# Moving a convolution block ahead of the last pair of heads, and conv work beside the second triangular solve

## The chip, the core and the metric

The kernel runs on one NeuronCore of a Trainium2 chip, in one launch and in float32. Its engines are TensorE (PE, matmuls and transposes), VectorE (DVE), ScalarE (ACT), GpSimd (POOL) and SyncE (SP, which issues most transfers; ACT issues some). Each engine works through its own instructions in a fixed order and waits on semaphores for the others. The metric is the device time of one execution in microseconds (us); a profile of one execution shows the span from its first to its last instruction, in the same unit.

## What is computed

One decoder layer for a sequence of 1024 tokens and a width of 1024. Its inputs meet in one projection, whose columns feed two groups side by side: an RWKV-7 group of 8 heads of 64, and a convolution group of 512 channels.

```
h = rmsnorm(x);  p = h @ w_in
y_rwkv: token shift, decays, then per head
    S_t = S_{t-1} (diag(decay_t) + a_t b_t^T) + v_t k_t^T ;  y_t = S_t r_t
    group norm, bonus, gate
y_conv: u * sigmoid(g), causal convolution with 31 taps, layer norm, silu
x = x + concat(y_rwkv, y_conv) @ w_out
x = x + relu(rmsnorm(x) @ w_ff1)^2 @ w_ff2
y = rmsnorm(x)
```

## The kernel before

Tokens lie in 16 chunks of 64. The recurrence is turned into small matrix products per chunk, for which a triangular system must be solved. The work comes in these parts; the names are those of the functions in the code.

- `mix_block` and `in_proj`: a block of 128 columns of the input projection, in two halves of 512 tokens. Each half takes 48 matmuls of 128x256 (three products of rounded halves of float32, eight slices of the width, two pieces). Eight heads make four pairs; each pair needs three such blocks (k, r and v). While the recurrence runs, their accumulators are the PSUM banks `cb` and `yb`, in turn.
- `conv_block`: two such blocks (value and gate) for 128 channels, so four halves. The product with the gate goes to the tile `h2`, of which there is one (`H2B = 1`); its first instruction is a memset of a border (`h` in the profile, L309). The convolution is 47 multiply-adds on DVE (`taps`, L328 to L331) and a join, which `do_taps(n)` issues in portions of n/31 of them. The weights of a block are loaded to one raw buffer and split by ACT and DVE (`load_w`, L219, L220).
- `decays` and `stage1`: for one pair and one half of the sequence, the decays, scaled keys (`AR`, `KB`), their products with a mask (`AM`, L471), and transposed copies, which are stored to DRAM for the recurrence (`lk_d`, `am_d`, `v_d`, `n2_d`).
- `solve`: for a group g of two pairs, DVE loads `Q` from `am_d`, inverts 128 small triangles of 32 in 60 steps (L528, L530) and stores them to `qd_d`. `merge` joins the triangles by two rounds of small products on PE (`QT,MX` and `QS,PT`) and stores the result to `th_d`.
- `step(g)`: one chunk of the recurrence of group g. `fetch` loads `LK`, `rhs` and `TA`; `chain` then runs hops of four matmuls of 64x64 on PE (eight in the trace): `rhs,LK`, a copy `SR` on ACT, `SR,TA` (the product with Th), a copy `rhs` on ACT, `rhs,LK` again and a sum on DVE (L624). Two more hops write the output. Group 0 uses the banks `ca` and `ya`, group 1 `cb` and `yb`. Each group has 16 chunks.
- `conv_norm(h)`: the layer norm and silu of the convolution for one half of the tokens; transposes on PE, the rest on ACT and DVE. It needs all taps of all four blocks. Its pool `sc` is opened and closed around it.
- `load_wout`: output weights, through two raw buffers (`woraw`, `RB = 2`), rounded by ACT (`woh`, L716) and completed by DVE (`wol`, L717). `out_first(t, n)`: 24 matmuls of 128x256 for the conv half of the output projection of 128 tokens and 512 columns; DVE adds the input (L724). `out_second(t)` adds the head half, after `post(d)` has normed and gated the recurrence's output.
- Then come the MLP (`early`, `Pair`) and its second product; they are not touched.

The order of the instructions on each engine is found when the kernel is built: a scheduler takes the operations in the order of the code as their priority and places each where its operands are expected to be there. `solve` and `merge` of both groups and `step(0)` stand one level (`HP = 4000`) ahead of their place, `step(1)` two levels. So the code's order of calls decides what is at hand when an engine would wait. Taps that are issued after a `solve` in the code are placed behind its last step (`gate`).

Of the kernel before, what the change touches and what calls it, by code (L numbers as in the profile page):

```python
# [52 lines left out]
def hymba_layer(ctx: ExitStack, tc: tile.TileContext, a: dict, out: bass.AP):  # L53
# [85 lines left out]
    cv_ctx = tc.tile_pool(name="cv", bufs=1)  # L139
# [41 lines left out]
    def prm(name, i=0, n=1):  # L181
        j, o = off[name]
        return pars[j][:, o + i:o + i + n]
# [30 lines left out]
    def load_w(c0):  # L214
        raw = wp.tile([P, 8, P], F32, name="wraw", bufs=1)
        nc.sync.dma_start(out=raw, in_=w_in_d[:, :, c0:c0 + P])
        wh = wp.tile([P, 8, P], F32R, name="wh")
        wl = wp.tile([P, 8, P], F32R, name="wl")
        S.activation(wh, raw, AF.Copy)  # L219
        V.tensor_tensor(wl, raw, wh.bitcast(F32), op=ALU.subtract)  # L220
        return wh, wl
# [80 lines left out]
    taps = []  # L302
    gate = {"solve": None}

    def conv_block(cb):
        tag = in_banks[-1]
        wg, wu = load_w(CG + cb * P), load_w(CU + cb * P)
        h2 = hc.tile([P, 3, 16 + 512], F32, name="h2", bufs=H2B)
        V.memset(h2[:, :, 0:16], 0.0)  # L309
        for h in range(2):  # L310
            bg = in_proj(wg, h * 512, 512, tag)
            th = hc.tile([P, 512], F32, name="th", bufs=1)
            S.activation(th, bg, AF.Tanh, scale=0.5)
            bu = in_proj(wu, h * 512, 512, tag)
            o = slice(16 + h * 256, 16 + h * 256 + 256)
            V.scalar_tensor_tensor(h2[:, 0:2, o].rearrange("p e n -> p n e"), th.rearrange("p (n e) -> p n e", e=2), 1.0,
                                   bu.rearrange("p (n e) -> p n e", e=2), op0=ALU.add, op1=ALU.mult)
            V.tensor_tensor(h2[:, 2, o], h2[:, 0, o], h2[:, 1, o], op=ALU.add)
        acc = accs[cb] = cv.tile([P, 2, 512], F32, name="acc", bufs=4)
        odd = mp.tile([P, 513], F32, name="odd", bufs=1)  # L320

        def tap(ph, i):

            o, c = ((acc[:, 0], cw[:, 2 * i, cb:cb + 1]), (odd[:, 1:513], cw[:, max(2 * i - 1, 0), cb:cb + 1]), (acc[:, 1], cws[:, i, cb:cb + 1]))[ph]
            x = h2[:, ph, i + 1:i + 1 + 512]
            if ph == 1 and i == 1:
                V.memset(odd[:, 0:1], 0.0)
                return V.tensor_scalar(o, x, c, None, op0=ALU.mult)  # L328
            if i == 0:
                return V.tensor_scalar(o, x, c, prm("conv_b", cb) if ph == 0 else cb2[:, cb:cb + 1], op0=ALU.mult, op1=ALU.add)  # L330
            return V.scalar_tensor_tensor(o, x, c, o, op0=ALU.mult, op1=ALU.add)  # L331

        def join(*_):
            V.tensor_tensor(acc[:, 1], acc[:, 1], acc[:, 0], op=ALU.subtract)
            V.tensor_tensor(acc[:, 1], acc[:, 1], odd[:, 1:513], op=ALU.subtract)
            return V.tensor_tensor(acc[:, 0], acc[:, 0], odd[:, 0:512], op=ALU.add)

        taps.extend((tap, (ph, i)) for ph in (0, 2, 1) for i in range(ph == 1, 16))
        taps.append((join, ()))
# [3 lines left out]
    def do_taps(n):  # L343
        tapped[0] += n
        for f, j in taps[:tapped[0] * 48 // TAPS - tapped[1]]:
            i = f(*j)
            if gate["solve"] is not None:
                tc.add_manual_dep(i.ins, gate["solve"].ins.name, NOSYNC, reason="solve first")
        n = tapped[0] * 48 // TAPS - tapped[1]
        tapped[1] += n  # L350
        del taps[:n]
# [3 lines left out]
    def mix_block(blk, hs):  # L355
        w = load_w(blk * P)
        for h in hs:
            pm = m0.tile([P, 513], F32, name="pm")
            if h == 0:
                V.memset(pm[:, 0:1], 0.0)  # L360
            else:
                S.copy(pm[:, 0:1], carry[:, blk:blk + 1])
            mx = mp.tile([P, 512], F32, name="rkv"[blk // 4], bufs=2)
            mixed(blk, h * 512, 512, pm, 0, w, mx)
            if h == 0:
                S.copy(carry[:, blk:blk + 1], pm[:, 512:513])
            mixes[blk, h] = mx
# [133 lines left out]
    def solve(g, hs):  # L501
        with tc.high_priority(offset=SOLVE_HP[g] * HP):
            solve_blocks(g, hs)
# [205 lines left out]
    def load_wout(pool, raws, ks):  # L709
        for n in range(2):  # L710
            for k in ks:
                raw = raws.tile([P, 512], F32, name="woraw", bufs=RB)
                nc.sync.dma_start(out=raw, in_=w_out_d[:, k, n * 512:(n + 1) * 512])
                wh = pool.tile([P, 512], F32R, name=f"woh{k}{n}")
                wl = pool.tile([P, 512], F32R, name=f"wol{k}{n}")
                S.activation(wh, raw, AF.Copy)  # L716
                V.tensor_tensor(wl, raw, wh.bitcast(F32), op=ALU.subtract)  # L717
                wos[k, n] = wh, wl
# [7 lines left out]
    def out_first(pool, t, n):  # L726
        xr = pool.tile([P, 512], F32, name="xr", bufs=2)
        nc.sync.dma_start(out=xr, in_=x_d[t * P:(t + 1) * P, n * 512:(n + 1) * 512])
        i, cT = slice(t % 4 * P, (t % 4 + 1) * P), cTs[t // 4]
        onto(t, n, [((cT[k][0][:, i], cT[k][1][:, i]), wos[4 + k, n]) for k in range(4)], xr)  # L730

    def out_second(t):
        y = yos.pop(t)
        for n in range(2):
            onto(t, n, [((y[0][:, k], y[1][:, k]), wos[k, n]) for k in range(NP)], x2[t][:, n * 512:(n + 1) * 512])

    def step(g):

        c = steps[g]
        steps[g] += 1  # L740
        d = c // 2
        with tc.high_priority(offset=(1 + g) * HP):
            if c == 0:
                fetch(g, 0)
                fetch(g, 1)
            if c < 14:
                fetch(g, c + 2)
            if c % 2 == 0:
                ys[g] = bank("ya" if g == 0 else "yb")
            chain(g, c, ys[g])  # L750
            if c % 2 == 1:
                z = ys[g].t[:, 0:256].rearrange("p (n t) -> p n t", n=4)
                if g == 1 and d >= DIRECT:
                    ybufs[d] = op.tile([P, 8, C], F32, name="y", bufs=2)
                    nc.sync.dma_start(out=ybufs[d][:, 0:4], in_=y_d[:, 0, d])
                    S.copy(ybufs[d][:, 4:8], z)
                else:
                    y = cp.tile([P, 4, C], F32, name="y", bufs=1)
                    S.copy(y, z)
                    nc.sync.dma_start(out=y_d[:, g, d], in_=y)  # L760

    def ready(pool, d):

        if d not in ybufs:
            ybufs[d] = pool.tile([P, 8, C], F32, name="y", bufs=2)
            for g in range(2):
                nc.sync.dma_start(out=ybufs[d][:, 4 * g:4 * g + 4], in_=y_d[:, g, d])
# [243 lines left out]
    stage1(2, 0)  # L1011
    decays(2, 1)
    stage1(2, 1)
    do_taps(16)
    decays(3, 0)
    step(0)
    mix_block(7, (0, 1))
    mix_block(3, (0, 1))
    step(0)
    mix_block(11, (0, 1))  # L1020
    do_taps(15)
    step(0)
    stage1(3, 0)
    decays(3, 1)
    step(0)
    stage1(3, 1)
    step(0)
    conv_block(3)
    do_taps(8)
    step(0)  # L1030
    solve(1, (0, 1))
    step(0)
    merge(1, 0)
    step(0)
    do_taps(23)
    assert not taps
    step(0)
    merge(1, 1)
    step(0)
    done_in()  # L1040
    cycles["any"] = ("ps", "ps", "ps", "pr")
    ct = open_pool("ct", side="right")
# [3 lines left out]
    step(0)  # L1046
    wo = open_pool("wo", side="right")
    load_wout(wo, wo, (4, 5, 6, 7))
    step(0)
    step(1)  # L1050
    step(0)
    step(1)
    step(0)
    sc = open_pool("sc", side="right")
    cTs[1] = conv_norm(sc, ct, 1)
    close_pool("sc")
    sv_ctx.__exit__(None, None, None)
    out_first(wo, 2, 1)
    step(1)
    cv_ctx.__exit__(None, None, None)  # L1060
    nx = open_pool("nx")
    op = open_pool("op")
    load_wout(op, op, (0, 1, 2, 3))
    step(0)
    step(0)
    assert steps[0] == 16
    cycles["any"] = ("ps", "ca", "ps", "ya", "ps", "pr")
    out_first(wo, 0, 0)
    step(1)
    ready(op, 0)  # L1070
    post(op, 0)
    out_first(wo, 1, 0)
    out_first(wo, 2, 0)
    out_first(wo, 0, 1)
    out_first(wo, 3, 0)
    out_second(0)
    step(1)
    step(1)
    ready(op, 1)
    post(op, 1)  # L1080
    out_first(wo, 3, 1)
    out_first(wo, 1, 1)
    ready(op, 2)
    post(op, 2)
    out_first(wo, 4, 0)
    out_second(1)
    out_first(wo, 5, 1)
    out_first(wo, 5, 0)
    step(1)
    out_first(wo, 6, 0)  # L1090
    step(1)
    ready(op, 3)
    post(op, 3)
    out_second(2)
    out_first(wo, 7, 0)
    out_first(wo, 4, 1)
    step(1)
    out_first(wo, 7, 1)
    out_first(wo, 6, 1)
# [260 lines left out]
```

## Time and profile before

| | us |
|---|---|
| median of 3 runs | 1291.79 |
| lowest, highest | 1289.95, 1292.08 |
| profiled execution | 1291.95 |
| its span | 1290.2 |
| PE busy in it | 1217.5 (94%) |
| DVE busy | 944.8 (73%) |
| ACT busy | 558.0 (43%) |
| mean granted clock of PE | 0.961 |

The page cuts the span into 40 slices of 32.3 us; each digit is the busy share in tenths, and PEclk the clock granted to PE in tenths of full speed. Matmuls overlap: the start-to-start time of two is their cost in a row, not the duration that each row gives. A row of the time-ordered views has the start, the duration, the engine, the line, the operation with its operands (out<-in), the shapes and, in brackets, the idle time ahead of it and who ended it. An operation of the chain of work that ended last is a step of what set the end.

### The profile page before, as it was taken

The numbers are of one execution on the slowest core, as the hardware profiler recorded it, in microseconds if no ns is written. First come the engines' busy times: TensorE is split into PE (matmuls) and PEld (weight loads), VectorE is DVE, ScalarE is ACT, GpSimd is POOL, SyncE is SP. The second block draws the span as 40 slices with busy tenths as digits, with TensorE's granted clock in tenths as the row PEclk, the third lists the DMA queues.
The fourth block names the chain that finished last, engine by engine and source line by source line (L and its number), as shares of the span: only waits on it lengthen the run. The fifth ranks groups of instructions, "written<-read, shape, count | busy, mean of one in ns | idle before, by whom it ended". The sixth has DMA issues, their size and how long they took to land.

```text
span 1290.2 us, 20800 instructions
## 1 busy us (share of the span) xinstructions
PE 1217.5 (94%) x8107; PEld 1052.2 (82%) x8107; DVE 944.8 (73%) x1639; ACT 558.0 (43%) x1001; POOL 107.4 (8%) x57
## 2 busy tenths in 40 slices
PE   5999999998999688999999899999997999999996
PEld 4999898887888577999988788888876788888885
DVE  6479696789549945664668766665459898897997
ACT  6432433333441166333468455455562333333344
POOL 1000000000000000000000000000015234242310
PEclk9999999997997586999999999999999999999999
DMA  5213426455464555734225454443276425232003
GB/s 191 58 50 98 125 62 176 113 139 123 118 168 130 129 143 165 216 111 123 78 88 184 152 164 153 150 146 109 87 268 217 142 66 164 65 101 79 17 1 131
DMA packets 194475, 161.44 MB, mean 125 GB/s; under 512 B 54386, under 2 KB 153784, under 8 KB 194376
## 3 DMA queue, kind: packets, MB, share of 16 engines
q1 hardware_dynamic: 181192, 157.90, 41.5%
q10 hardware_dynamic: 13056, 2.13, 0.9%
q8 instruction: 64, 1.05, 0.3%
q14 instruction: 35, 0.29, 0.1%
q0 software_dynamic: 128, 0.08, 0.0%
HBM read 110.23 MB, written 49.84 MB: 124 GB/s over the span
## 4 chain that ended last, share of the span: by engine, by line
PE 61%; DVE 9%; DMA 4%; ACT 2%; issue 1%; SPq 0%; ACTq 0%; DVEq 0%
PE ps L96 27%; PE yb L96 9%; PE ya L96 8%; PE cb L96 7%; PE ca L96 6%; PE pr L96 3%; DVE bl L852 2%; DVE al L852 2%; DVE sA L1190 1%; DVE x L1221 1%; PE ps L99 1%; DMA woraw<-in_w_out_dram 1%; DMA th_d<-QS 1%; DVE Q L530 1%; DVE Qt L528 1%
## 5 line engine op out<-in xcount | busy, mean ns | idle before, releaser
L851 ACT ACTIVATE ah<-sA 128x1024 fp32r<-128x1024 f32 x32 | 33.9, 1061 | 120.9 <-PE yb L96 48.0
L96 PE MATMUL cb<-hh,wh 128*128 128x256 f32 x248 | 72.8, 293 | 1.5 <-ACT hh L243 1.5
L96 PE MATMUL cb<-hl,wh 128*128 128x256 f32 x248 | 73.0, 294 | 0.3 <-DVE hl L244 0.3
L96 PE MATMUL cb<-hh,wl 128*128 128x256 f32 x248 | 71.8, 290 | 0.0
L96 PE MATMUL ps<-bh,ah 128*128 128x512 f32 x168 | 64.5, 395 | 5.6 <-ACT ah L851 3.5
L96 PE MATMUL ps<-bh,al 128*128 128x512 f32 x168 | 65.0, 391 | 3.2 <-DVE al L852 3.2
L96 PE MATMUL ps<-bl,ah 128*128 128x512 f32 x168 | 66.3, 395 | 1.5 <-DVE bl L852 1.5
L96 PE MATMUL yb<-hh,wh 128*128 128x256 f32 x232 | 67.7, 292 | 0.0
L96 PE MATMUL yb<-hh,wl 128*128 128x256 f32 x232 | 66.6, 287 | 0.0
L96 PE MATMUL yb<-hl,wh 128*128 128x256 f32 x232 | 66.5, 287 | 0.0
L851 ACT ACTIVATE w1h<-s 128x512 fp32r<-128x512 f32 x64 | 40.3, 632 | 52.6 <-PE ps L96 34.0
L852 DVE TENSOR_TENSOR al<-sA,ah 128x1024 fp32r<-128x1024 f32 x32 | 48.0, 1506 | 19.6 <-ACT ah L851 19.5
L852 DVE TENSOR_TENSOR w1l<-s,w1h 128x512 fp32r<-128x512 f32 x64 | 44.0, 688 | 24.8 <-ACT w1h L851 24.7
L1190 POOL TENSOR_TENSOR sB<-B,B11e 128x1024 f32<-128x1024 f32 x4 | 12.5, 3134 | 541.6 <-DVE al L852 539.3
L96 PEld LDWEIGHTS cb<-hh,wh 128*128 128x128 f32 x248 | 48.5, 195 | 5.4 <-ACT hh L243 1.9
L871 ACT ACTIVATE c<-c 128x512 f32<-128x512 f32 x60 | 37.9, 632 | 33.4 <-DVE c L957 20.1
L96 PEld LDWEIGHTS cb<-hl,wh 128*128 128x128 f32 x248 | 48.3, 195 | 4.8 <-issue 4.0
L96 PEld LDWEIGHTS cb<-hh,wl 128*128 128x128 f32 x248 | 48.2, 194 | 2.3 <-issue 2.1
L851 ACT ACTIVATE w1h<-w1r 128x512 fp32r<-128x512 f32 x48 | 30.2, 631 | 42.5 <-PE ps L96 26.6
L852 DVE TENSOR_TENSOR w1l<-w1r,w1h 128x512 fp32r<-128x512 f32 x48 | 32.9, 688 | 19.7 <-ACT w1h L851 19.7
L96 PEld LDWEIGHTS yb<-hh,wh 128*128 128x128 f32 x232 | 44.6, 192 | 3.1 <-issue 2.1
L96 PEld LDWEIGHTS yb<-hh,wl 128*128 128x128 f32 x232 | 44.6, 192 | 1.6 <-issue 1.5
(472 smaller groups left out, 4029.4 us busy)
## 6 DMA issues: line engine op xcount, KB each, us to landing
w1r<-in_w_ff_dram SPq DMA_DIRECT2D x44, 512.0 KB
hid_d<-c SPq DMA_DIRECT2D x64, 256.0 KB
LK<-lk_d SPq DMA_DIRECT2D x32, 384.0 KB
A<-hid_d SPq DMA_DIRECT2D x24, 512.0 KB
B<-in_w_ff_dram SPq DMA_DIRECT2D x24, 512.0 KB
wraw<-in_w_in_dram SPq DMA_DIRECT2D x22, 512.0 KB
xt<-in_x_dram SPq DMA_DIRECT2D x8, 512.0 KB
lk_d<-AR SPq DMA_DIRECT2D x16, 256.0 KB
```

The costliest lines, as they stand in the source:

```text
L96: return self._order(PE.matmul(o, lhsT=lhsT, rhs=rhs, start=start, stop=stop, skip_group_check=more))
L99: self._order(PE.transpose(o, in_, identity))
L528: V.tensor_tensor(o, Q[:, 0:s, s:s + 1].to_broadcast([R, s, n]), Q[:, s:s + 1, s + 1:32].to_broadcast([R, s, n]), op=ALU.mult)
L530: V.tensor_tensor(Q[:, 0:s, s + 1:32], Q[:, 0:s, s + 1:32], o, op=ALU.add)
L851: S.activation(hi, src, AF.Copy)
L852: V.tensor_tensor(lo, src, hi.bitcast(F32), op=ALU.subtract)
L871: S.activation(c, c if src is None else src, AF.Relu)
L1190: engine.tensor_tensor(t, x, y, op=op)
L1221: V.tensor_tensor(o, o, banks[t].t, op=ALU.add)
```

## The change

Three things move; no operation is added or taken away.

1. `conv_block(3)` stands ahead of the mixes of pair 3 instead of behind its `stage1`. All taps of block 2 are issued ahead of it (31 of 31 instead of 16), and all of block 3's ahead of the second solve instead of 23 of 31 behind it. The steps of group 0 are spread differently among these.
2. `conv_norm(0)`, the weights of the conv half and three `out_first` stand between the second group's merges and its first step; `conv_norm(1)` comes before step 0 of group 1 as well.
3. Further `out_first` are interleaved with the steps of both groups, one or two for each, and `out_second` and `post` follow in a different order.

```diff
-    do_taps(16)
+    do_taps(31)
     decays(3, 0)
     step(0)
+    conv_block(3)
+    step(0)
     mix_block(7, (0, 1))
+    step(0)
+    do_taps(8)
     mix_block(3, (0, 1))
     step(0)
     mix_block(11, (0, 1))
-    do_taps(15)
-    step(0)
+    step(0)
+    do_taps(8)
     stage1(3, 0)
     decays(3, 1)
     step(0)
     stage1(3, 1)
     step(0)
-    conv_block(3)
-    do_taps(8)
-    step(0)
+    do_taps(15)
+    assert not taps
     solve(1, (0, 1))
     step(0)
     merge(1, 0)
     step(0)
-    do_taps(23)
-    assert not taps
-    step(0)
     merge(1, 1)
-    step(0)
     done_in()
...
     load_wout(wo, wo, (4, 5, 6, 7))
-    step(0)
-    step(1)
-    step(0)
-    step(1)
+    out_first(wo, 0, 0)
+    step(0)
+    out_first(wo, 1, 0)
+    out_first(wo, 2, 0)
     step(0)
     sc = open_pool("sc", side="right")
     cTs[1] = conv_norm(sc, ct, 1)
     close_pool("sc")
     sv_ctx.__exit__(None, None, None)
+    cv_ctx.__exit__(None, None, None)
+    out_first(wo, 0, 1)
+    step(1)
+    step(0)
+    out_first(wo, 1, 1)
     out_first(wo, 2, 1)
     step(1)
-    cv_ctx.__exit__(None, None, None)
+    step(0)
+    out_first(wo, 3, 0)
     nx = open_pool("nx")
     op = open_pool("op")
     load_wout(op, op, (0, 1, 2, 3))
-    step(0)
+    step(1)
+    step(0)
+    out_first(wo, 3, 1)
     step(0)
...
-    out_first(wo, 0, 0)
     step(1)
     ready(op, 0)
     post(op, 0)
-    out_first(wo, 1, 0)
-    out_first(wo, 2, 0)
-    out_first(wo, 0, 1)
-    out_first(wo, 3, 0)
-    out_second(0)
-    step(1)
-    step(1)
+    out_first(wo, 4, 0)
     ready(op, 1)
     post(op, 1)
...
```

What this does to the engines' order, at three places. First PE, between the first group's merge (`ya<-QS,PT`) and the projections that follow it; `kd`, `cbm`, `r` and `lt` are operands of stage one and of the decays. Before:

```order
 L96 MATMUL ya<-QS,PT 32x32 x32
 L99 MATMUL ps<-ident,kd 128x128 x4
 L96 MATMUL ps<-cbm,v 128x128 x4
 L96 MATMUL ps<-r,bones 128x512
 L96 MATMUL cb<-hh_151,wl 128x256
 L96 MATMUL cb<-hh_155,wh 128x256
```

Now:

```order
 L96 MATMUL ya<-QS,PT 32x32 x32
 L99 MATMUL ps<-ident,kd 128x128 x4
 L96 MATMUL ya<-rhs,LK 64x64 x4
 L99 MATMUL ps<-ident,kd 128x128
 L96 MATMUL ps<-cbm,v 128x128 x4
 L99 MATMUL ps<-ident,kd 128x128 x3
 L96 MATMUL ca<-rhs,LK 64x64 x4
 L96 MATMUL ya<-rhs,TA 64x64 x4
 L96 MATMUL ps<-r,bones 128x512
 L96 MATMUL ps<-lt,wup 128x512
 L96 MATMUL ca<-rhs,LK 64x64 x4
```

Projections of pair 3 (`cb<-hh,wh` and so on) stood among these; now hops of group 0 do, and the next projection, the last half of block 3, comes only after its fourth chunk has begun.

Then PE beside the second solve. Before, hops of group 0 alone:

```order
 L96 MATMUL ca<-rhs,LK 64x64 x4
 L96 MATMUL ya<-rhs,LK 64x64 x4
 L96 MATMUL ca<-SR,TA 64x64 x4
 L96 MATMUL ca<-rhs,LK 64x64 x4
 L96 MATMUL ya<-rhs,TA 64x64 x4
```

Now, where `yc` are the normed conv rows that are transposed back, and `woh` and `cvh` the operands of the conv half of the output projection:

```order
 L96 MATMUL ca<-rhs,LK 64x64 x4
 L96 MATMUL ya<-rhs,LK 64x64 x4
 L99 MATMUL ps<-ident,yc_4850 128x128 x3
 L99 MATMUL ps<-ident,yc_4851 128x128 x3
 L99 MATMUL ps<-ident,yc_4852 128x128 x3
 L99 MATMUL ps<-ident,yc_4853 128x128 x3
 L99 MATMUL ps<-ident,yc_4850 128x128
 L99 MATMUL ps<-ident,yc_4851 128x128
 L99 MATMUL ps<-ident,yc_4852 128x128
 L99 MATMUL ps<-ident,yc_4853 128x128
 L96 MATMUL ps<-woh_5004,cvh_4921 128x256 x3
```

The conv norm of the first half and three chunks of output have moved there, and group 0's last chunks behind the solve.

Last DVE, near the end of that solve. Before:

```order
 L528 TENSOR_TENSOR Qt<-Q 128x168
 L530 TENSOR_TENSOR Q<-Q,Qt 128x24x7
 L528 TENSOR_TENSOR Qt<-Q 128x150
 L530 TENSOR_TENSOR Q<-Q,Qt 128x25x6
 L624 TENSOR_TENSOR rhs<-ca,SR 64x256
 L528 TENSOR_TENSOR Qt<-Q 128x130
```

Now:

```order
 L530 TENSOR_TENSOR Q<-Q,Qt 128x26x5
 L717 TENSOR_TENSOR wol_5017<-woraw,woh_5016 128x512
 L528 TENSOR_TENSOR Qt<-Q 128x108
 L717 TENSOR_TENSOR wol_5023<-woraw,woh_5022 128x512
 L530 TENSOR_TENSOR Q<-Q,Qt 128x27x4
 L528 TENSOR_TENSOR Qt<-Q 128x84
 L531 MEMSET Q 128x32
 L530 TENSOR_TENSOR Q<-Q,Qt 128x28x3
 L528 TENSOR_TENSOR Qt<-Q 128x58
 L530 TENSOR_TENSOR Q<-Q,Qt 128x29x2
 L528 TENSOR_TENSOR Qt<-Q 128x30
 L530 TENSOR_TENSOR Q<-Q,Qt 128x30
```

Splits of output weights stand between the solve's steps, where taps of block 3 stood between earlier ones.

More of the change, by code (lines that the diff above doesn't have):

```diff
@@ L1071, in hymba_layer @@
     post(op, 0)
-    out_first(wo, 1, 0)
-    out_first(wo, 2, 0)
-    out_first(wo, 0, 1)
-    out_first(wo, 3, 0)
+    out_first(wo, 4, 0)
+    ready(op, 1)
+    post(op, 1)
+    out_first(wo, 5, 0)
     out_second(0)
     step(1)
+    out_first(wo, 4, 1)
     step(1)
[L1079 to L1082, printed above, removed]
     ready(op, 2)
     post(op, 2)
-    out_first(wo, 4, 0)
     out_second(1)
+    step(1)
     out_first(wo, 5, 1)
-    out_first(wo, 5, 0)
-    step(1)
     out_first(wo, 6, 0)
@@ L1095, in hymba_layer @@
     out_first(wo, 7, 0)
-    out_first(wo, 4, 1)
     step(1)
```

## The prediction

> **What bounds the kernel now.** I read the page's slices first, then the busy time by stretch, then the chain that ended last, then single instructions in order of time.
>
> ```profile
> span 1290.2 us, 20800 instructions
> PE   5999999998999688999999899999997999999996
> DVE  6479696789549945664668766665459898897997
> PEclk9999999997997586999999999999999999999999
> ```
>
> TensorE (PE) is full nearly everywhere; the clock drops only in slices 10 and 13 to 16 (counted from 1). The busy times of those places (columns: stretch, its length, PE, PEld, DVE, ACT, POOL busy, granted clock, DMA share, GB/s):
>
> ```profile
> 304.00:320.00 16.00, 16.00 (x201) 14.43 (x199) 16.00 (x27) 4.54 (x14) 0.11 (x1) 0.57 0.56 122
> 320.00:400.00 80.00, 79.93 (x708) 69.34 (x706) 45.81 (x92) 30.16 (x68) 0.11 (x1) 1.00 0.56 141
> 400.00:512.00 112.00, 86.76 (x1008) 75.39 (x1009) 81.05 (x184) 45.95 (x93) 0.30 (x1) 0.68 0.53 140
> 512.00:720.00 208.00, 203.47 (x1540) 184.27 (x1539) 140.82 (x345) 103.25 (x225) 0.00 (x0) 0.99 0.47 141
> ```
>
> From 320 to 400 and from 512 on, PE is the bound. Between 400 and 512 it is idle for 25 us and runs at 0.68 of its clock: 86.76 x 0.68 = 59 us of work in 112, so 53 us are lost there. That is the pot that the change aims at. The chain there (start, us, what):
>
> ```profile
> 378.89 4.43 DMA am_d<-AM
> 383.34 4.68 DMA Q<-am_d
> 388.05 1.24 DVE Q L524
> 422.66 1.24 DVE Q L532
> 423.91 3.21 DMA qd_d<-Q
> 427.15 4.15 DMA QS<-qd_d
> 438.51 1.48 SPq L542
> 440.03 2.56 DMA th_d<-QS
> 444.69 1.09 PE cb L96 x8
> 506.40 5.38 PE ps L96 x33
> ```
>
> The second solve starts at 388.05, takes VectorE (DVE) 35.9 us to 423.9, and its merge lets the second group's recurrence begin at 444.69. The output projection makes PE dense only at 506.4. All PE work is in both kernels; the time therefore changes by when PE becomes dense, plus the work that is still left at that point.
>
> **The change, part by part.** Prices first: a tap and its neighbour, projection matmuls at full and at half clock, one hop of the recurrence at each clock, and the start and end of a DVE stretch.
>
> ```profile
> 286.31 0.45 DVE L547 STREAM_TRANSPOSE QT<-QS 128x256 f32<-128x256 f32 x1 [2.26 <-DMA QS<-qd_d]
> 300.92 0.74 DVE L331 SCALAR_TENSOR_TENSOR acc<-h,cw,acc 128x512 f32<-128x512 f32 x1
> 301.58 0.74 DVE L331 SCALAR_TENSOR_TENSOR acc<-h,cws,acc 128x512 f32<-128x512 f32 x1
> 324.69 0.10 DVE L309 MEMSET h<- 128x48 f32 x1
> 329.35 0.28 PE L96 MATMUL yb<-hl,wh 128*128 128x256 f32 x1
> 329.47 0.28 PE L96 MATMUL yb<-hh,wl 128*128 128x256 f32 x1
> 315.22 0.41 PE L96 MATMUL cb<-hh,wh 128*128 128x256 f32 x1
> 315.43 0.41 PE L96 MATMUL cb<-hl,wh 128*128 128x256 f32 x1
> 334.36 0.68 PE L96 MATMUL ca<-SR,TA 64*64 64x64 f32 x8
> 408.15 1.11 PE L96 MATMUL ca<-rhs,LK 128*64 128x64 f32 x8 [0.46 <-ACT rhs L619]
> ```
>
> By successive starts a tap costs 0.66 us, a projection matmul 0.12 (0.21 at half clock); a hop takes PE 0.61 (1.05).
>
> (a) Block 3 goes ahead of pair 3's mixes. It needs h2, of which there is one buffer, so its gate product waits until block 2's last tap. From the first merge's transpose to that point DVE now runs 64 instructions: 38 taps x 0.66, 2 scans of 1.14, one weight split of 1.13, the rest 0.05 to 0.66, 40.2 us. Counted the same way, the stretch before comes to 38.5 against 38.4 in the trace (286.31 to 324.69). So PE's projections resume at 286.3 + 40.2 = 327. Until then PE holds only stage one of pair 2 (7.3 us), the merges (1.5) and 16 hops of group 0 (9.8), 18.6 us in the 28 from 299. Before, projection matmuls lay in this gap too. Bounds: 325 (the chunk work falls behind it) and 333 (the chunks, whose copies queue on ScalarE (ACT), hold DVE up). The loads of block 3's weights on SP come earlier too; they cost nothing, since the taps cover them.
>
> (b) From there 7 half-blocks of 48 matmuls follow without a break: 336 x 0.12 = 40.3, with 21 hops x 0.61 = 12.9 and one norm of 0.9, 54.1; 5 more for the first half-clock windows and one bank that waits. DVE has 53 us in the same stretch, 48 taps among them, so neither waits long. End at 386.5 (bounds 383 and 393).
>
> (c) Then stage one of pair 3, both halves, with no projection left beside it. Rows for its path:
>
> ```profile
> 352.65 0.69 DVE L471 TENSOR_TENSOR AM<-ps,mask 128x512 f32<-128x512 f32 x1 [0.75 <-PE ps L96]
>   ACT kt L485: 8.9, 2
> ```
>
> The second row is from the waits on am_d: ACT, which issues half of the loads of Q, stands 4.4 us for each half until am_d has landed, and pair 3's second decays are queued behind. From the first half's last mask (353.3) to the solve's start the trace has 34.7 us. Now: masks end at 391.9; 4.4 for am_d on ACT; two tanh, sum, scan, exponentials and seven DVE products (0.60 to 0.66 each) 7.4, partly overlapped; the products on PE, and beside them the norm with its trip through DRAM and the chunk hops between, 7.6; masks end at 411.3; then 9.2 (378.9 to 388.05). Start at 420.5. Bounds: 411 (no queueing on ACT and PE) and 424.
>
> (d) The solve. Of the 35.9 us before, 11 taps, block 3's gating and 12 chunk steps were 13.1, so the solve alone is 22.7. Now the taps are gone, but conv norm 0, five weight splits and chunk work stand between its steps: 4 statistics, 4 gates, 4 + 5 splits at about 0.61 by start, 12 small steps of 0.2, 6 chunk steps of 0.34 and some aggregates, 15.3. Sum 38.0. The splits bring a wait:
>
> ```profile
> 475.39 1.28 DVE L689 SCALAR_TENSOR_TENSOR hn<-th,hn 128x512 f32<-128x512 f32 x2
> 488.21 0.69 DVE L717 TENSOR_TENSOR wol<-woraw,woh 128x512 fp32r<-128x512 f32 x1
> 486.06 4.85 DMA woraw<-in_w_out_dram
> 498.96 3.68 DMA woraw<-in_w_out_dram
> ```
>
> There are two raw buffers: a split frees one, the load takes 3.7 to 4.9 us, ACT's rounding 0.6. The third split stands 2.3 us of DVE work behind the second one, the fifth 2.5 behind the fourth. Each waits some 2.5 us with the solve's last steps behind it: 5. Solve end 420.5 + 38.0 + 5 = 463.5, 39.6 later than before. Bounds of the wait: 0 and 8. On SP seven of these loads now stand ahead of the stores of Q; the last of them is released by the fifth split, before Q is done, so they delay nothing. On ACT's queue the rounding copies stand there likewise; POOL has no part in it.
>
> (e) Merge and first chunk: before, 423.9 to 444.69 is 20.8 to the first Th product. Here the four MX loads that delayed th_d on SP (the row at 438.51) are issued earlier: 18 (bounds 16 and 21), and 4.5, four hops and a copy, to the point where output matmuls fill PE. Dense at 486, 20.4 before 506.4.
>
> (f) What is left at that point. Before, 42 hops of both recurrences and 381 output matmuls of the conv half; now 86 hops and 312. Difference: 44 x 0.61 = +26.9, 69 x 0.12 = -8.3, half a merge and one gate product +1.8: +20.4. The three output chunks beside the solve are thus 8.6 us of PE work only; the bounds are 18 and 23.
>
> (g) Between 486 and the end of group 1's chain four hops follow their predecessor with nothing between, and five more have under 1 us. Before there was none. At 0.5 to 1 us each: +3.5 (0 to 10).
>
> Sum: -20.4 + 20.4 + 3.5 = +3.5 on the profiled execution's 1291.95 (span 1290.2, 1.75 around it; the runs' median of 1291.79 lies 0.16 below): 1295.5. The gain at the gap is real, but it only moves recurrence work, which no longer lies beside conv work, behind the solve.
>
> **A rule weighed.** Columns as in the second table:
>
> ```profile
> 404.00:412.00 8.00, 7.52 (x65) 6.68 (x64) 7.77 (x17) 1.47 (x4) 0.00 (x0) 0.50 0.60 164
> 417.00:424.00 7.00, 5.14 (x69) 4.25 (x67) 6.52 (x22) 1.18 (x4) 0.30 (x1) 0.99 0.55 143
> 424.00:444.00 20.00, 10.75 (x200) 9.64 (x200) 18.75 (x32) 2.21 (x6) 0.00 (x0) 0.50 0.57 132
> ```
>
> With hops alone the clock was 0.50 at 94% busy and 0.99 at 73%; so I take half clock wherever (a) and (d) have hops alone. The Trainium skill, "TensorE: Matmul & The Clock Gate", Part 1: The HAM clock gate, says that the clock halves after an idle window of about 3.4 us and is full again after one busy window. By that rule the stretch 404 to 412, whose idle gaps are below half a microsecond, should have been at full clock; the trace does not agree, and the measurement stands.
>
> **The rivals.**
> 1. Faster: the solve starts early. For it: 320 to 400 shows PE, not latency, pacing the mixes, and without projections behind the PE queue stage one could run straight through. Against: ACT's 4.4 us behind am_d stay. At a start of 411 the sum is 9.5 lower, 1286. It decides at 414: each microsecond there is one in the end.
> 2. The clock stays full, since transposes and output matmuls stand among the hops. Saved on the path: 30 matmuls x 0.09 in (b), 2.7; two merge products x 0.3 and three or four hops x 0.44, 2.1: 1290.7, no change.
> 3. Much slower: group 1's chain becomes the bound after 481.5, its first Th product.
>
> ```profile
> 444.69 1.08 PE L96 MATMUL cb<-SR,TA 64*64 64x64 f32 x8 [4.45 <-DMA TA<-th_d]
> 500.33 0.68 PE L96 MATMUL cb<-SR,TA 64*64 64x64 f32 x8 [0.50 <-ACT SR L613]
> 616.01 0.68 PE L96 MATMUL cb<-SR,TA 64*64 64x64 f32 x8
> ```
>
> Six chunks took 55.6 us from 444.69, 9.3 each, beside conv norm 1. PE's work from 486 to this chain's end is 85 hops (51.9), 312 conv output matmuls (37.4), 288 of the head half (34.6), 48 of the first MLP block (5.8), transposes, gate products and a merge (13.7): 143.4, so the chain ends at 486 + 143.4 + 3.5 = 633. That leaves 633 - 481.5 - 4 = 147.5 us for 15 chunks, 9.8 each. At 10.5 it ends 10 us later: 1305.5. For it: the margin is 5%. Against: ACT's conv work is done by then.
>
> **How the numbers follow.** A difference under 0.2% (2.6 us; the three runs span 2.1) can't be told from none: faster is below 1289.2, slower above 1294.4. Forecast 0.42 (own range 1291 to 1300: 0.30 slower, 0.12 same). Rival 1 0.27 (0.26 faster, 0.01 same), rival 2 0.15 (0.11 same, 0.03 faster, 0.01 slower), rival 3 0.16, all slower. Sums: faster 0.29, same 0.24, slower 0.47. The range reaches from rival 1 with no wait in (d), 1281, to rival 3; a tenth is left out at either side: 1282 to 1306.
>
> **What would show it.** (a) PE's projections resume within 325 to 333, right after the memset of h. (c) The first step of the second solve at 411 to 424. (d) Two waits of DVE on the weight halves inside the solve, and its last product near 464. (e) PE dense from about 486. (f) A second group's chain that ends near 633, 17 us after the 616.01 of now. Wrong would be: a solve that ends before 455, or a chain whose chunks take over 10 us.

## The result and the profile after

The changed kernel takes 1308.26 us (median of 4 runs, 1304.14 to 1310.09) against 1291.93 for the one before: a ratio of 1.0124, 95% interval 1.0096 to 1.0152. It is 1.2% slower; the forecast was 1295.5, with a range up to 1306. A later series of 4 runs gave 1307.29 and 1.0127 (1.0107 to 1.0147). The profiled execution took 1307.13.

The page of the changed kernel, the rows that answer to those of before:

```profile
span 1305.4 us, 20820 instructions
PE   5999999998997669899999999999997999999996
PEclk9999999998897768899999999999998999999998
```

The hole of PE is still there, in slices 13 to 15 (counted from 1), and the clock is low in slices 10, 11 and 13 to 17. The stretch of the hole (columns as before: stretch, length, PE, PEld, DVE, ACT, POOL busy, granted clock, DMA share, GB/s):

```profile
400.00:512.00 112.00, 78.17 (x800) 64.40 (x799) 64.74 (x169) 50.35 (x94) 0.30 (x1) 0.70 0.54 135
```

The pot of 53 us between 400 and 512 did not shrink: 78.17 x 0.70 = 55 us of work in 112, so 57 are lost. Finer stretches show where the 15.2 us between the two profiled executions lie. First before, then after:

```profile
300.00:340.00 40.00, 36.23 (x364) 30.91 (x364) 35.60 (x60) 16.88 (x40) 0.11 (x1) 0.83 0.55 127
470.00:512.00 42.00, 32.62 (x266) 27.23 (x266) 23.10 (x52) 31.33 (x57) 0.00 (x0) 0.76 0.53 152
512.00:560.00 48.00, 48.00 (x440) 45.70 (x439) 30.17 (x76) 17.69 (x42) 0.00 (x0) 1.00 0.61 187
610.00:660.00 50.00, 48.90 (x356) 44.30 (x355) 34.72 (x101) 26.54 (x60) 0.00 (x0) 1.00 0.22 67
700.00:740.00 40.00, 36.57 (x154) 29.54 (x154) 31.39 (x50) 21.38 (x38) 0.00 (x0) 0.96 0.49 158
960.00:1060.00 100.00, 90.14 (x384) 72.03 (x383) 93.41 (x79) 34.86 (x37) 38.94 (x12) 0.98 0.50 164
```

```profile
300.00:340.00 40.00, 35.26 (x380) 28.59 (x379) 29.96 (x51) 12.67 (x30) 0.11 (x1) 0.74 0.58 137
470.00:512.00 42.00, 32.67 (x476) 28.80 (x475) 20.66 (x49) 20.42 (x37) 0.00 (x0) 0.72 0.53 126
512.00:560.00 48.00, 43.55 (x424) 40.27 (x422) 21.02 (x53) 15.25 (x36) 0.00 (x0) 0.93 0.64 191
610.00:660.00 50.00, 47.62 (x446) 42.66 (x445) 33.35 (x102) 23.34 (x56) 0.00 (x0) 0.97 0.33 88
700.00:740.00 40.00, 40.00 (x186) 33.08 (x185) 36.79 (x60) 28.71 (x54) 0.00 (x0) 1.00 0.63 197
960.00:1060.00 100.00, 88.33 (x373) 70.95 (x372) 81.48 (x69) 37.59 (x44) 34.08 (x11) 0.97 0.55 189
```

Length minus PE busy x clock is what PE lost in a stretch. 300 to 340: 9.9 before, 13.9 after (+4.0). 400 to 512: 53 and 57 (+4). 512 to 560: 0 and 7.5. 610 to 660: 1.1 and 3.8 (+2.7). 700 to 740: 4.9 and 0 (-4.9). 960 to 1060, deep in the MLP: 11.7 and 14.3 (+2.6). The sum is +16, near the 15.2 (the mean clock of a stretch makes this rough by a microsecond or two).

The chain through the hole, after (start, us, what):

```profile
398.09 4.25 DMA am_d<-AM
414.89 4.95 DMA y_d<-y
419.87 2.39 DMA nup<-n_d
423.79 3.30 DMA am_d<-AM
427.46 4.19 DMA Q<-am_d
470.87 1.23 DVE Q L532
486.05 3.31 DMA th_d<-QS
489.43 2.10 DMA TA<-th_d
491.66 1.08 PE cb L96 x8
```

The second solve starts at 431.7 and is over at 472.1; before it was 388.05 to 423.9. On the way there stands a trip that the forecast had only beside other work: the key norms (n_d) go to DRAM behind the store of y on SyncE's queue. Two rows of DVE and some of PE in time order:

```profile
422.38 0.18 DVE L521 TENSOR_SCALAR nup<-nup 128x32 f32<-128x32 f32 x1 [4.21 <-DMA nup<-n_d]
423.08 0.68 DVE L471 TENSOR_TENSOR AM<-ps,mask 128x512 f32<-128x512 f32 x1
```

```profile
483.97 3.02 PE L99 MATMUL ps<-ident,yc 128*128 128x128 f32 x12 [0.28 <-ACT yc L679]
491.66 1.08 PE L96 MATMUL cb<-SR,TA 64*64 64x64 f32 x8 [4.67 <-DMA TA<-th_d]
492.67 1.11 PE L99 MATMUL ps<-ident,yc 128*128 128x128 f32 x4
...
540.53 1.08 PE L96 MATMUL cb<-rhs,LK 128*64 128x64 f32 x8 [2.71 <-DVE yo L652]
```

DVE waits 4.2 us for the norms, with the last mask of stage one (L471) queued behind them; the last part of am_d cannot be stored before that mask. (In a second trace of the same kernel, after_again, the wait is 1.49 us and the masks wait for PE in its place; the solve starts at 430.5.) And PE stands 4.67 us for the load of TA, at the second group's first Th product, with the last four transposes of the second conv norm behind it in its queue. All further output chunks stand behind those transposes in PE's order.

### The profile page after: what moved, and what is told of

It reads as the page before. It is cut to its first block, busy times and chain, and to the rows that moved or that the text cites. A ratio compares the mean times of both kernels' runs of the same rounds, so it can differ in the third digit from the quotient of the medians.

```text
span 1305.4 us, 20820 instructions
## 1 busy us (share of the span) xinstructions
PE 1218.9 (93%) x8107; PEld 1050.4 (80%) x8107; DVE 946.2 (72%) x1639; ACT 561.5 (43%) x1001; POOL 103.8 (8%) x57
## 3 DMA queue, kind: packets, MB, share of 16 engines
q8 instruction: 64, 1.05, 0.3%
## 4 chain that ended last, share of the span: by engine, by line
PE 81%; DVE 8%; DMA 7%; ACT 3%; issue 1%; SPq 1%; ACTq 0%; DVEq 0%
PE ps L96 29%; PE yb L96 14%; PE cb L96 12%; PE ya L96 11%; PE ca L96 8%; PE pr L96 4%; PE ps L99 2%; DVE bl L852 1%; DVE al L852 1%; DMA lk_d<-kt 1%; DMA am_d<-AM 1%; DMA Q<-am_d 1%; DMA qd_d<-Q 1%; DVE x L1221 1%; DVE sA L1190 1%
## 5 line engine op out<-in xcount | busy, mean ns | idle before, releaser
L852 DVE TENSOR_TENSOR al<-sA,ah 128x1024 fp32r<-128x1024 f32 x32 | 51.7, 1618 | 19.5 <-ACT ah L851 19.4
```

What stands on the lines that cost most here:

```text
L852: V.tensor_tensor(lo, src, hi.bitcast(F32), op=ALU.subtract)
```

## The experiments

All ratios are to the kernel before, run on the same chip beside the experiment.

**The two halves of the change apart.** block_alone keeps the conv block ahead and puts back the order of before from the merges on; output_alone does the reverse. The step(0) at the seam keeps their number at 16.

```diff
block_alone, against the changed kernel:
     merge(1, 1)
+    step(0)
     done_in()
...
output_alone, against the kernel before:
     merge(1, 1)
-    step(0)
     done_in()
...
```

> The early conv block alone: the changed part up to the merges, then the order of before (no output chunk beside the solve; the sixteen steps of group 0 as before). Theory L (all of the loss comes from the second solve, which now starts at 431.7 instead of 388 and drags everything behind it): the solve starts within 2 us of 431.7 and the time is 13 to 18 us above before. Rival theory H (about half of it comes from the placement of the output chunks, behind which the first group's chain halts from 440 to 504 and then runs beside the second group's): the solve starts as late, but the time is only 3 to 9 us above before, and there is no stall of PE near 540.

> The new order of output chunks and steps alone, with the conv block, its taps and the second solve where they were before. Theory L: the solve starts at 388 as before, so the time is within 3 us of before. Theory H: the last steps of group 0 fall beside the first ones of group 1 again, PE stands for some us there, and the time is 3 to 8 us above before.

Measured: block_alone 1311.19 us, 1.0135 (1.0115 to 1.0156); output_alone 1297.77, 1.0043 (1.0028 to 1.0058). The solve starts at 431.6 in the first and at 387.5 in the second. So the early block costs 1.35% by itself, 18.8 us, near theory L's 13 to 18; but it also loses 6.4 us of PE from 512 to 560, where theory H expected no stall without the new output order. That order costs 0.4% without the block, 5.4 us, as theory H had it and not L's 3 at most; with the block it changes nothing that can be told from the noise (1.0135 against 1.0124 and 1.0127). Two rows, block_alone first, then output_alone:

```profile
470.00:512.00 42.00, 26.63 (x423) 23.09 (x424) 16.09 (x36) 17.07 (x32) 0.00 (x0) 0.58 0.49 112
512.00:560.00 48.00, 39.19 (x335) 37.15 (x334) 25.53 (x66) 21.56 (x39) 0.00 (x0) 0.89 0.52 160
```

Without output chunks beside the solve PE does 26.63 x 0.58 = 15 us of work in the 42 before 512 (before 25, changed 24). With the chunks used there, and the solve early, PE is short of work 40 us later: in output_alone it loses 13 us of the 48 from 512, 7 of them in one wait:

```profile
551.26 2.08 PE L96 MATMUL pr<-sg,wgu 128*128 128x128 f32 x8 [6.96 <-DVE yo L653]
```

**The norms' trip.**

```diff
-        nc.sync.dma_start(out=n2_d[p // 2, h, ...
+        (nc.scalar if p == 3 else nc.sync).dma_start(out=n2_d[p // 2, h, ...
```

> The changed kernel, but the store of the key norms of the last pair is issued on ScalarE's queue, right behind the copy that makes them, instead of on SyncE's queue behind the store of y. If the wait of VectorE on the norms' trip (4.2 us, with the last mask of stage one behind it) sets the start of the second solve, the solve starts 4 to 5 us earlier, near 427, and theory L expects the time 4 to 5 us below the changed kernel, theory H 2 to 5. If the masks would have waited for PE anyway, the start moves less than 1.5 us and the time is the same.

> The kernel before with the norm store of the last pair on ScalarE's queue. In its trace the norms' trip lies beside projections: the theory that the trip hurts only where stage one stands alone expects the time of before within 2 us. If the store's place was a cost of its own all along, it is 4 us or more below before.

Measured: 1298.31 us, 1.0037 (1.0021 to 1.0053), 10 us below the changed kernel; in the kernel before, 1292.36 and 1.0004 (0.9989 to 1.0018). The first product of the solve (earliest and last of the group: here one instruction) in norm_store_act and in the changed kernel:

```profile
L524 DVE TENSOR_TENSOR Q<-Q,nup x1: 1224/1224/1224, 426.4 to 426.4; 128x1024 f32<-128x1024 f32 x1
L524 DVE TENSOR_TENSOR Q<-Q,nup x1: 1226/1226/1226, 431.7 to 431.7; 128x1024 f32<-128x1024 f32 x1
```

The start moves 5.3 us in this pair of traces, a little more than expected, and the time moves by twice that. But 1.7 of the 5.3 lie ahead of the trip (the third mask of the second half is at 415.75 against 417.48), and other traces give less: the solve starts at 426.4 to 431.9 in the five kernels with the early block whose norm store is on ScalarE's queue, and at 429.1 to 431.7 in the six traces of those without. By the means of these traces the trip is worth some 2 us on the start (an estimate; their other edits differ too), and the time did not move by that alone. The trip is free in the kernel before, where projections lie beside stage one.

**The steps of the first group.** In the changed kernel group 0's chain halts between its 13th and 14th Th product (440.3 and 503.9). norm_and_steps has the norm store as well.

```diff
     load_wout(wo, wo, (4, 5, 6, 7))
+    step(0)
+    step(0)
+    step(0)
+    step(0)
+    step(0)
+    step(0)
     out_first(wo, 0, 0)
-    step(0)
     out_first(wo, 1, 0)
     out_first(wo, 2, 0)
-    step(0)
...
```

The other four that this replaces stand further down.

> The changed kernel, but the six last steps of group 0 stand ahead of the first output chunk, so that its chain runs on beside the solve and is over when group 1's begins. Theory H: the halt of the chain from 440 to 504 and the stall of PE near 540 are gone, and the time is 7 to 12 us below the changed kernel (1296 to 1301). Theory L: the steps add VectorE work beside the solve, which ends some 2 us later, and the time is that of the changed kernel within 3 us.

> The norm store on ScalarE's queue and the six steps of group 0 ahead of the output chunks, both in the changed kernel. If the two repairs act on different places (the start of the second solve; the halt of the first group's chain), their gains of 10 and 8 us add and the time is 1289 to 1293, that of before. If both only shorten the same gap before group 1's chain can begin, the time is that of the norm store alone, 1296 to 1300.

Measured: steps_early 1300.60 us, 1.0074 (1.0053 to 1.0094); norm_and_steps 1297.17, 1.0042 (1.0024 to 1.0059). In steps_early the halt is gone (last Th product of group 0 at 452.0), and the time is 8 us lower; the two gains do not add. In norm_and_steps the solve starts at 431.9 again: the norms come early, and the masks now wait for PE, where hops at half clock stand between their products. And the stretch from 512 to 560 still loses 6.8 us in steps_early, where group 0 had been done for 60 us. So the part of theory H that put the stall near 540 down to the two chains running together falls.

**Loads of Q, and raw buffers.** norm_and_q_sync has the norm store and the first edit, raw_four the second alone.

```diff
-                (nc.sync, nc.scalar)[bl].dma_start(out=Q[p0:p0 + 32], ...
+                (nc.sync, nc.sync if g else nc.scalar)[bl].dma_start(out=Q[p0:p0 + 32], ...
...
-                raw = raws.tile([P, 512], F32, name="woraw", bufs=RB)
+                raw = raws.tile([P, 512], F32, name="woraw", bufs=4 if ks[0] == 4 else RB)
```

> As the run with the norm store on ScalarE's queue, and in the second solve the two loads of Q that ScalarE issues are issued by SyncE, so that ScalarE no longer stands 4 us in front of the second half's decays until am_d has landed. If that stand is on the path to the solve, as step (c) of the prediction had it, the solve starts 3 to 5 us earlier than 426.4 and the time is 3 to 6 us below 1298. If SyncE's queue, which then waits for am_d itself, holds the stores of stage one back, the start stays within 1.5 us or comes later.

> The changed kernel with four raw buffers for the weights of the conv half's output projection instead of two. Step (d) of the prediction priced the waits on them at 5 us; the trace of the changed kernel shows 1.6 us of waits on the weight splits before the solve's last product, and PE stands 2.9 us at 463 for one. By step (d) the solve (431.7 to 470.9) is 5 us shorter and the time 4 to 7 us lower; by the trace it is 1 to 2.5 us shorter and the time 0 to 3 us lower.

Measured: norm_and_q_sync 1296.44 us, 1.0042 (1.0024 to 1.0059), solve start 428.1, no earlier than the 426.4 of norm_store_act. Either ScalarE's stand behind am_d is not on the path, or SyncE's queue, which now waits for am_d itself, takes its place; the run can't tell. raw_four 1299.69, 1.0054 (1.0035 to 1.0073), over 8 us below the changed kernel, though its solve is not shorter (first to last product 429.9 to 472.4, against 431.7 to 470.9). Neither theory has that. What raw_four shares with norm_store_act and steps_early is an order on PE: the planner put all transposes of the second conv norm ahead of group 1's first Th product, while in the changed kernel four stand behind it. norm_and_steps has the order of the changed kernel there and gains as much, so it is not the only way to that time: its trace loses as much PE from 470 to 512 (18.3 us against 18.5) and 8.8 less in 430 to 470, 512 to 560 and 610 to 660 together.

**The order around the second conv norm.**

```diff
-    cTs[1] = conv_norm(sc, ct, 1)
+    with tc.high_priority(offset=HP):
+        cTs[1] = conv_norm(sc, ct, 1)
```

> The changed kernel, with the second conv norm given the priority of a merge: up to the second solve's end every engine's order is the same, and then the norm's eight groups of transposes stand ahead of the second group's first Th product on PE, no longer behind it. In the changed kernel's trace that product stands 4.7 us for its load at half clock, with the transposes and the next output chunk behind it, and the runs norm_store_act and raw_four both had the transposes first. If this order is what these two have in common, the time is 7 to 9 us below the changed kernel (1298 to 1301), with the solve at 431 as before it; the later solve then accounts for the remaining 7 us or less. If the earlier solve was the cause of the gain of norm_store_act, the time here is within 3 us of the changed kernel.

> The changed kernel itself again, on the same chip as the run with the second norm first, to compare the two directly. Expected within 2 us of its 1308.3 and 1.2% above before; if it is several us lower, part of the gains of the experiments is a difference between chips or runs.

Measured: 1299.03 us, 1.0065 (1.0048 to 1.0082), beside 1307.29 for the changed kernel on the same chip. That is 8.3 us, with the solve at 429.1 (430.5 in the trace of after_again). PE around that place in norm1_first:

```profile
485.38 0.66 PE L99 MATMUL ps<-ident,yc 128*128 128x128 f32 x4
486.72 0.39 PE L96 MATMUL ps<-woh,cvh 128*128 128x256 f32 x1 [0.68 <-ACT th L688]
489.30 0.68 PE L96 MATMUL cb<-SR,TA 64*64 64x64 f32 x8
```

The load of TA takes as long as ever, but PE does output chunks meanwhile, and at full clock. The stretches from 480, norm1_first and then the changed kernel:

```profile
480.00:497.00 17.00, 14.95 (x238) 12.84 (x238) 7.83 (x15) 12.71 (x22) 0.00 (x0) 0.85 0.48 107
497.00:512.00 15.00, 15.00 (x155) 13.79 (x146) 4.68 (x9) 3.37 (x8) 0.00 (x0) 1.00 0.80 205
```

```profile
480.00:497.00 17.00, 11.06 (x217) 8.82 (x207) 6.14 (x21) 10.18 (x17) 0.00 (x0) 0.50 0.51 91
497.00:512.00 15.00, 15.00 (x191) 14.09 (x188) 6.40 (x13) 5.98 (x12) 0.00 (x0) 0.83 0.40 117
```

14.95 x 0.85 + 15.00 = 27.7 us of work against 11.06 x 0.50 + 15.00 x 0.83 = 18.0: a mean of 0.83 over 15 us is half clock to 502. (The priority changes PE's order from this place on also further down.)

The priority turns ScalarE's order round as well. ACT at that place, first in the changed kernel, then in norm1_first:

```profile
489.45 0.42 ACTq L545 DMA_DIRECT2D QS<-qd_d  x1
489.92 0.78 ACT L687 ACTIVATE hn<-ps,clbh,clgh 128x512 f32<-128x512 f32 x1 [3.50 <-DMA th_d<-QS]
490.60 0.77 ACT L688 ACTIVATE th<-ps,clbh,clgh 128x512 f32<-128x512 f32 x1
491.92 0.78 ACT L688 ACTIVATE th<-ps,clbh,clgh 128x512 f32<-128x512 f32 x1
```

```profile
483.88 0.78 ACT L687 ACTIVATE hn<-ps,clbh,clgh 128x512 f32<-128x512 f32 x1 [0.31 <-PE ps L99]
484.56 0.77 ACT L688 ACTIVATE th<-ps,clbh,clgh 128x512 f32<-128x512 f32 x1
485.88 0.78 ACT L688 ACTIVATE th<-ps,clbh,clgh 128x512 f32<-128x512 f32 x1
486.26 0.42 ACTq L545 DMA_DIRECT2D QS<-qd_d  x1
```

L545 loads QS, of which there is one buffer, for the merge's second half; it can't be issued before the first half's th_d is stored, at 489.4 in the changed kernel. There it stands ahead of hn and th, which read the transposes out of their PSUM banks, and ACT stands 3.50 us; in norm1_first two pairs of hn and th go first. The last four transposes begin 0.05 us after the first th ends in norm1_first (485.33 and 485.38), and so they do in raw_four, norm_store_act, steps_early and the three kernels that combine repairs and have the transposes first. In norm_and_q_sync and norm_and_raw the trace names this th as what they wait for, which points to a bank that th sets free. In the changed kernel that th ends at 491.37, only 0.3 us before the Th product. An estimate from these rows: with PE's order alone turned round, the transposes would begin at 491.4 instead of 492.7, and the next output chunk, which in norm1_first begins when the second th has ended, at 492.7 instead of 497.0, not at the 486.7 of norm1_first. The two orders turn together in every trace, norm_and_steps with both as in the changed kernel, so what each costs is not shown; the run shows what both cost together with the changes further down.

**Together.** three_repairs has the norm store, the early steps and four raw buffers, norm_and_raw the first and the last; their edits are those shown. In both all transposes stand ahead of the product.

> The changed kernel with the norm store on ScalarE's queue, the six steps of group 0 ahead of the output chunks and four raw buffers; on PE all transposes of the second conv norm then stand ahead of group 1's first Th product, which they did not in norm_and_steps. If the order of the transposes is a cost of its own, worth 8 us, it comes on top of the gain of norm_and_steps: 1287 to 1291, below before or equal to it. If all these repairs recover the same time, the result is that of norm_and_steps, 1295 to 1299.

> The changed kernel with the norm store on ScalarE's queue and four raw buffers, the steps left where they are. Both of its parts alone have the transposes ahead of the Th product and stood at 0.4 and 0.5% above before. If that order is what they share, together they gain nothing over the norm store alone: 0.2 to 0.5% above before. If the buffers and the norm's trip each had a gain of their own, it is at before or below, under 0.1%.

Measured: 1299.91 us, 1.0054 (1.0035 to 1.0073), and 1299.12, 1.0056 (1.0033 to 1.0079). Most of what the repairs recover is the same time: each alone, and all together, end 0.4 to 0.7% above before. No version beat the kernel before.

## Why the prediction was wrong

The sign was right, the size was not: +3.5 us forecast, +16 measured. The sign is not all luck: the 3.5 were step (g), and every kernel with the early block does lose 5 to 9 us of PE from 512 to 560, where the one before loses none. But most of the measured size comes from steps to which the forecast gave no loss. By its own steps:

- **(a) held, at its late end.** Projections resume at 332.4 (327 forecast, bounds 325 to 333), 1.4 us after the memset of h:

```profile
324.07 0.42 DVE L624 TENSOR_TENSOR rhs<-ca,SR 64x256 f32<-64x256 f32 x1 [1.95 <-PE ca L96]
330.98 0.10 DVE L309 MEMSET h<- 128x48 f32 x1
332.40 0.58 PE L96 MATMUL cb<-hh,wh 128*128 128x256 f32 x1
```

  The step counted DVE as never idle; it stood 3.8 us for chunk hops and decays in three places, the longest shown.
- **(b) held:** 56.9 us from there to the end of the last projection at 389.3 (59.1 and 386.5 forecast; 327 and 59.1 make 386.1).
- **(c) failed in size:** 431.7 against 420.5, past the bound of 424. Of the 11.2 us, 2.8 are (a) and (b) together. The masks of the first half took 0.5 longer. ScalarE then resumed 7.7 us after the last of them (395.15 to 402.81) instead of 4.4, since the store of am_d, behind that of y on SyncE's queue, was issued only at 398.09. From there to the end of the second half's last mask, at 423.76, it took 21.0 instead of 15.0; 4.2 of these are DVE's wait for the norms' trip, which the step had counted within 7.6 us of work on PE. The last part took 8.0 instead of 9.2. In after_again the wait for the norms is 1.5 and the start 430.5, past the bound too.
- **(d) held as a sum:** 40.4 us (43 forecast). The two waits of 2.5 on the weight splits measured 0.88, 0.43 and 0.24 before the last product, 1.6 instead of 5; the solve beside the norm took 38.8 for 38.0. raw_four took those waits' cause away and the solve got no shorter.
- **(e) is the step that failed.** The first Th product came 19.6 us after the solve's end, within the 16 to 21 forecast. But the step took PE as full 4.5 us later, at 486, on the silent premise that hops and output chunks would interleave as data came. In the changed kernel two queues stand there: ScalarE's 3.50 us, for the load of QS ahead of the second conv norm's activations, and PE's 4.67 us, for the load of TA ahead of the last four transposes. The output chunks come behind both, and the half clock lasts to 502, 30 us after the solve. norm1_first, with both orders the other way round, has its chunks begin at 486.7, 17 us after its solve, and is 8.3 us faster. In that series the changed kernel ends 17.2 us above the kernel before and norm1_first 8.9, where the forecast had 3.5: these orders, with what the priority moves further down, are 8.3 of the 13.7 us by which it missed there. Which of the two queues costs how much stays open; the rows above speak for ScalarE's. Both stood in the program's order, but the forecast had not looked for them.
- **(f)** can't be read off as one number. The last hop of group 1 begins at 654.9 (chain end near 633 forecast), later by the 8 of (e), by (g) and by the solve.
- **(g) was mis-sized:** 3.5 forecast, 0 to 10 as bounds; PE lost 7.5 us from 512 to 560 and 2.7 more from 610 to 660 than before. A wait of 2.7 us costs more than itself, since the clock halves after it (below).
- **Not foreseen:** a gap near 717 before the MLP, 4.9 us, is closed in every kernel with the early block, and the MLP's own gaps near 1000 cost 2.6 more.

Rival 1 (an early start of the solve) and rival 2 (a full clock) did not come. Rival 3's mark did: group 1's Th products go from 491.7 to 653.7, 10.8 us a chunk, over the limit of 9.8. But its mechanism did not bound the kernel: from 560 to 610 PE was busy 49.9 of 50 us, and norm1_first, 10.3 us a chunk, is 8 us faster. As far as these figures tell, the chain was late because it waited for PE, not PE for it.

What stays open: how the 8.3 us divide between the two queues, why every repaired version ends at 0.4 to 0.7% and none lower, why norm_and_steps gains as much with both orders unturned, and what the stall near 537 to 541 waits for. The trace names DVE, which had long written what the hop reads; a load of LK issued at 536.2 fits better. LK's ring of three buffers and those of rhs and TA (two) are shared by both groups; no run has a fourth LK buffer.

## What to carry to other kernels

A piece of work moved out of a latency chain leaves the chain bare: here the stage behind it grew a wait for a DRAM trip (1.5 to 4.2 us) and a wait for a store in a queue (3.3) that the projections had covered for nothing. Where a planner sets the order, read on every engine what stands behind each instruction that will wait for a DMA, loads that a computing engine issues among them; here a hop on PE and a load on ScalarE stood ahead of the second conv norm, and the run that turned both round gained 8.3 us, more than the whole forecast. And when unlike repairs each give 8 to 10 us and together 8 to 12, their gains must not be added: most of what they recover is the same time.

## What the hardware showed

One short wait of PE can cost nearly twice its length. The stall near 540 of the changed kernel, cut into five stretches, in each of which the clock has one value:

```profile
533.00:536.40 3.40, 3.40 (x37) 3.13 (x36) 1.38 (x2) 1.25 (x3) 0.00 (x0) 1.00 0.29 95
536.40:539.80 3.40, 1.42 (x19) 1.12 (x16) 1.24 (x3) 1.88 (x5) 0.00 (x0) 1.00 0.63 173
539.80:543.20 3.40, 2.09 (x16) 1.85 (x16) 1.42 (x3) 0.99 (x2) 0.00 (x0) 0.50 0.83 214
543.20:546.60 3.40, 3.40 (x17) 3.40 (x17) 0.25 (x1) 0.37 (x1) 0.00 (x0) 0.50 0.78 227
546.60:550.00 3.40, 3.40 (x31) 3.20 (x31) 0.00 (x0) 0.35 (x1) 0.00 (x0) 1.00 0.16 48
```

PE was busy 42% of the second stretch and 61% of the third; then it ran the third and the fourth at half clock, the fourth being full. 3.3 us of idle time in the two stretches cost 6.0 in all (3.4 x 3 less 1.42, 1.05 and 1.70 of work). The Trainium skill, "TensorE: Matmul & The Clock Gate", HAM oscillation — how this bites in real kernels, tells that a DMA wait can throttle PE again and that the next work then starts cold; the trace agrees that a wait of PE does so, though what this one was for is open. The same page of the Trainium skill, Part 1: The HAM clock gate, asks for an idle window of about 3.4 us; here a window 42% busy was enough.
